# Attention scores cut into key chunks of 1024, 1024 and 256 in place of three of 768

## Chip, cores, metric

The kernel runs on one core of one Trainium2 chip, as one launch. The metric is device time in microseconds (us), the median of repeated runs. All matrix products here are done on operands split in two (a high part rounded to fp32r, and the rest), so that fp32 accuracy comes from two or three passes of fast matmuls.

## What is computed

One layer of a hybrid backbone for 128 prompt tokens and 2048 latent tokens, width 1024: RMS norm and modulation, one input projection, differential attention (8 heads) beside a bidirectional state-space scan (16 heads), one output projection, residual and final norm. The change is in the latent tokens' attention: 2048 queries against 2304 keys (2048 latent, 256 cached), per head two softmax maps of 64 dimensions each and values of 128.

```python
def diff_attention(q, k, v, lam):              # 8 heads, c = 2 maps of 64 dims
    ...
        s = jnp.einsum('bqhcd,bkhcd->bchqk', qi, k).astype(F32) * scale
        p = jax.nn.softmax(s, axis=-1)
        a = p[:, 0] - lam * p[:, 1]
        return jnp.einsum('bhqk,bkhd->bqhd', a.astype(v.dtype), v)
...
def layer(...):
    ...
    att = diff_attention(q, k_all, v_all, lam)
    ...
    out = jnp.concatenate([att, ssd_y], axis=-1) @ w_out
    return x + gate * out, ...
```

## The kernel before

The program goes through projections (TensorE tile ps_p), the scan (ps_y, ps_cb), the latent attention, and the output projection (ps_f). The body does not issue instructions: it records them, and a planner puts them in order. `Plan.simulate` (L388) walks the recorded instructions with an assumed cost for each (`Plan.price`, L305) and, engine by engine, takes of those that are ready the one that is due first. The result is one fixed order for each engine, which the chip follows: an engine whose next instruction has to wait does nothing else. Every recorded instruction carries the line L233, so the tiles' names tell them apart.

The latent attention has 128 units: 8 heads by 16 query tiles of 128 rows; two consecutive units make a pair that shares its queries (256) and its values' output. `frame(i)` (L1617) records unit i's scores beside the later steps of earlier units:

- `s_chunk` (L1509): scores of one map (m = 0, 1) against one key chunk (j = 0, 1, 2). TensorE writes them into tile ps_s, from the pool psS (L1473), which has two buffers of two PSUM banks; queries' high part and rest are two passes over the same keys (high parts in partitions 0 to 63, rests in 64 to 127 of the key tile K). VectorE evicts the chunk with one instruction (TENSOR_SCALAR, in the profile TENSOR_SCALAR_CACHE_REDUCE) into the SBUF tile S of that map and takes the chunk's row maximum on the way. Six chunks make a unit: three of map 0, three of map 1. Since the pool has two buffers, the matmuls of each chunk wait for the eviction of the chunk before the last.
- `s_max`, `s_exp`: the maximum over the chunks (VectorE), the exponential with its sum (ScalarE).
- `combine` (L1534): VectorE makes one factor (tile sm) from the sums, GpSimd forms map 0 minus lambda times map 1, in three pieces of 768 columns.
- `t_high`, `t_low` (L1545): TensorE transposes the result, three blocks of 128 at a time, into ps_t (three buffers, shared with ps_q); ScalarE takes the high part (aH), VectorE the rest (aL).
- `av_kt` (L1567): per block of 128 keys three value matmuls of 256 columns into ps_o, for both units of the pair at once.

`load_k` (L1373) loads one key chunk as one tile K by two DMAs on SP's queue, high parts and rests; nine tiles of 768 keys hold one and a half heads. The planner's cost of a score matmul is columns / 2.4 + 3 ns.

Of the kernel before, what the change touches and what calls it, by code (L numbers as in the profile page):

```python
# [9 lines left out]
F32 = mybir.dt.float32  # L10
F32R = mybir.dt.float32r
# [7 lines left out]
P = 128  # L19
D = 1024  # L20
KT = D // P
SEQ = 128
# [445 lines left out]
def body(tc, I, O):  # L468
    pl = Plan(tc)
    nc = pl  # L470
    es = ExitStack()
    mm = nc.tensor.matmul
# [76 lines left out]
    def bank(tag):  # L549
        return psB.tile([P, 512], F32, tag=tag, name=f"ps_{tag}", bufs=(1 if tag == "cb" else 2))  # L550
# [163 lines left out]
    for m0 in range(0, 2 * D, 384):  # L714
        n = min(384, 2 * D - m0)
# [13 lines left out]
    for g, wm in enumerate(wms):  # L729
# [3 lines left out]
        n = min(384, 2 * D - g * 384)  # L733
        if g in (2, 5):
            for j in range(2):
# [7 lines left out]
                for f in range(n // P):  # L743
                    o = 2 * (g * 3 + f) + j
                    mm(pm[:, o:o + 1], lhsT=acc[:, f * P:(f + 1) * P], rhs=ones[:, 0:1], start=True, stop=True)
            continue
        ps = bank("y")
# [4 lines left out]
        for f in range(n // P):  # L752
            o = 2 * (g * 3 + f)
# [614 lines left out]
    kpool_cm = pl.tile_pool(name="kpool", bufs=1, side="right", reuse_waits="tile")  # L1368
    kpool = kpool_cm.__enter__()
    NG = NKEY // 768  # L1370
    Kt, Vt = {}, {}

    def load_k(h, m, j):  # L1373
        t = kpool.tile([P, 768], F32R, tag="K", name="K", bufs=9)
        for r, src in enumerate((kH_d, kL_d)):
            load(out=t[r * 64:r * 64 + 64].bitcast(F32),
                 in_=src[h, m * 64:m * 64 + 64, SEQ + j * 768:SEQ + (j + 1) * 768])
        Kt[h, m, j] = t

    def load_q(h, t):  # L1380
# [8 lines left out]
    for m in range(2):  # L1389
        for j in range(NG):  # L1390
            load_k(0, m, j)
# [82 lines left out]
    psS = psS_cm.__enter__()  # L1474
# [24 lines left out]
    def get_unit(i):  # L1499
        if i not in U:  # L1500
            u = U[i] = Obj()
            u.pr = get_pair(i // 2)
            u.h, u.c, u.qo = i // 16, 1 + i % 16, (i % 2) * P
            u.pool = spS if i % 4 < 2 else spT
            u.S, u.mx = {}, u.pool.tile([P, 2, 4], F32, tag="mx", name="mx", bufs=2)
            u.sm = u.pool.tile([P, 4], F32, tag="sm", name="sm", bufs=2)
        return U[i]

    def s_chunk(i, k):  # L1509
        u = get_unit(i)  # L1510
        m, j = k // NG, k % NG
        if j == 0:
            u.S[m] = u.pool.tile([P, NKEY], F32, tag=f"S{m}", name=f"S{m}", bufs=2)
        ps = psS.tile([P, 2, 512], F32, tag="S", name="ps_s")
        kt = Kt[u.h, m, j]
        for l in range(2):
            for a in range(2):
                mm(ps[:, a, :384], lhsT=u.pr.q[:, l, m, u.qo:u.qo + P], rhs=kt[:, a * 384:(a + 1) * 384],
                   start=l == 0, stop=l == 1)
        src, dst = ps[:, :, :384], u.S[m][:, j * 768:(j + 1) * 768]  # L1520
        nc.vector.tensor_scalar(out=dst.rearrange("p (a b) -> p a b", a=2), in0=src, scalar1=1.0, scalar2=None,
                                op0=ALU.mult, op1=ALU.max, accum_out=u.mx[:, m, j:j + 1])

    def s_max(i):
        u = U[i]
        for m in range(2):
            nc.vector.tensor_reduce(out=u.mx[:, m, 3:4], in_=u.mx[:, m, 0:NG], axis=AX.X, op=ALU.max, negate=True)

# [5 lines left out]
    def combine(i):  # L1534
# [3 lines left out]
                                op0=ALU.mult, op1=ALU.mult)  # L1538
        for j in range(NG):
            sl = slice(j * 768, (j + 1) * 768)  # L1540
# [76 lines left out]
    def frame(i):  # L1617
# [12 lines left out]
        for k in range(6):  # L1630
            if live:
                s_chunk(i, k)
                h, r = i // 16, i % 16
                if r == 15 and h + 1 < NH and k >= 3:
                    load_k(h + 1, 1, k - 3)
                if r == 5 and h + 1 < NH and k < 3:
                    load_k(h + 1, 0, k)
                if r == 6 and h + 1 < NH and k < 2:
                    load_v(h + 1, k, 0)
            if tl:  # L1640
                t_high(ti, k)
                t_low(ti, k)
            if k % 2 == 0:
                av((i - 3) * 3 + k // 2 - 1)
# [27 lines left out]
    spT = spT_cm.__enter__()  # L1672
    for g in range(NG):
        for l in range(2):
# [202 lines left out]
```

## Time and profile before

| | |
|---|---|
| median of 3 runs | 3106.76 us (3104.68, 3106.76, 3111.84) |
| the profiled execution | 3110.01 us |
| its span, first to last instruction | 3108.1 us |
| mean granted TensorE clock, share of full speed | 0.994 |
| TensorE busy | 3054.7 us, 98% |
| VectorE, ScalarE, GpSimd busy | 2305.7, 1836.8, 1327.8 us |
| score matmuls, first and last start | 1480.1 and 2687.4 us |

The busy time of matmuls counts overlapping ones once; a row with "xN" merges N instructions, and its mean (ns of one) includes the part in which the next matmul already runs. How far apart matmuls follow each other is read from the chain or from a count over a stretch. PEld is the loading of a matmul's stationary operand.

### The profile page before, as it was taken

What the parts mean: (1) busy time and instruction counts of PE and PEld (TensorE: products, weight loads), DVE (VectorE), ACT (ScalarE), POOL (GpSimd) and SP (SyncE); (2) the same over time, 40 slices, a digit from 0 to 9 for tenths busy, and PEclk for the clock granted to TensorE, in tenths of its full rate; (3) what the DMA queues carried; (4) which work ended last, traced back from release to release, by engine and by line L of the source; (5) the groups of instructions that cost most, each with busy time, mean ns of one, the idle gap of its engine ahead of it and who ended that gap; (6) DMA issues with size and microseconds to landing.
All of it is one profiled execution on the core that took longest, in us unless ns stands there. A gap on an engine that the chain in (4) does not pass through costs nothing.

```text
span 3108.1 us, 55843 instructions
## 1 busy us (share of the span) xinstructions
PE 3054.7 (98%) x20539; PEld 2899.4 (93%) x20539; DVE 2305.7 (74%) x4638; ACT 1836.8 (59%) x3258; POOL 1327.8 (43%) x1171
## 2 busy tenths in 40 slices
PE   8999999999999999999999999999999999989999
PEld 5899999998999999998999999999999999868887
DVE  5544524767685777754799999999999999877775
ACT  3233313333475667744688888888888888754442
POOL 2010100000021222210699999999999999700000
PEclk9999999999999999999999999999999999999999
DMA  8632422677687777759222222222223121286663
GB/s 287 213 122 91 139 79 96 195 237 235 219 266 242 235 235 247 240 164 215 78 61 76 67 66 65 67 66 65 68 68 77 55 71 35 90 277 199 176 203 96
DMA packets 481474, 449.25 MB, mean 145 GB/s; under 512 B 34447, under 2 KB 437160, under 8 KB 481202
## 3 DMA queue, kind: packets, MB, share of 16 engines
q1 hardware_dynamic: 479282, 445.52, 47.2%
q8 instruction: 162, 2.65, 0.4%
q14 instruction: 110, 0.90, 0.1%
q10 hardware_dynamic: 1920, 0.17, 0.0%
HBM read 305.96 MB, written 139.62 MB: 143 GB/s over the span
## 4 chain that ended last, share of the span: by engine, by line
PE 87%; DMA 4%; DVE 4%; SPq 2%; issue 1%; ACT 1%; POOL 1%; DVEq 0%; POOLq 0%; ACTq 0%
PE ps_p L233 32%; PE ps_s L233 17%; PE ps_o L233 13%; PE ps_t L233 8%; PE ps_f L233 5%; PE ps_v L233 5%; PE ps_y L233 4%; DMA yL<-y_d 2%; SPq L233 2%; DVE yx L233 1%; PE ps_tr L233 1%; DVE o L233 1%; PE ps_cb L233 1%; DMA vH_d<-vH 1%; POOL st L233 0%
## 5 line engine op out<-in xcount | busy, mean ns | idle before, releaser
L233 DVE TENSOR_SCALAR_CACHE_REDUCE S<-ps_s 128x768 f32<-128x768 f32 x768 | 726.7, 953 | 64.3 <-PE ps_s L233 49.1
L233 POOL TENSOR_TENSOR S<-S,S 128x768 f32<-128x768 f32 x384 | 710.5, 1878 | 5.0
L233 PE MATMUL ps_s<-K,q 128*128 128x384 f32 x3072 | 707.7, 348 | 0.4 <-DVE S L233 0.2
L233 PE MATMUL ps_p<-hH,wH 128*128 128x384 f32 (+1 forms) x2112 | 697.9, 330 | 0.0
L233 PE MATMUL ps_p<-hH,wL 128*128 128x384 f32 (+1 forms) x2112 | 690.8, 327 | 0.0
L233 PE MATMUL ps_p<-hL,wH 128*128 128x384 f32 (+1 forms) x2112 | 689.7, 327 | 0.0
L233 ACT ACTIVATE S<-S,mx 128x2304 f32<-128x2304 f32 x256 | 571.0, 2230 | 11.8 <-DVE mx L233 11.8
L233 PEld LDWEIGHTS ps_s<-K,q 128*128 128x128 f32 x3072 | 505.7, 189 | 2.6 <-DVE S L233 2.0
L233 PE MATMUL ps_o<-aH,V 128*128 128x256 f32 x2304 | 490.9, 286 | 0.0
L233 ACT CAST aH<-ps_t 128x384 fp32r<-128x384 f32 x768 | 348.1, 482 | 135.1 <-PE ps_t L233 131.8
L233 DVE TENSOR_TENSOR aL<-ps_t,aH 128x384 fp32r<-128x384 f32 x768 | 406.4, 550 | 25.7 <-ACT aH L233 21.6
L233 POOL TENSOR_SCALAR_AFFINE_SELECT ar<-ar 128x512 f32<-128x512 f32 x136 | 111.2, 825 | 704.8 <-ACT ea L233 663.8
L233 PEld LDWEIGHTS ps_p<-hH,wH 128*128 128x128 f32 x2112 | 398.6, 189 | 2.0 <-issue 1.2
L233 PEld LDWEIGHTS ps_p<-hL,wH 128*128 128x128 f32 x2112 | 398.7, 189 | 1.0 <-issue 0.8
L233 PEld LDWEIGHTS ps_p<-hH,wL 128*128 128x128 f32 x2112 | 398.4, 189 | 0.7 <-DVE wL L233 0.3
L233 POOL TENSOR_SCALAR S<-S,sm 128x768 f32<-128x768 f32 x384 | 347.2, 922 | 86.9 <-DVE sm L233 77.4
L233 PEld LDWEIGHTS ps_o<-aH,V 128*128 128x128 f32 x2304 | 381.1, 189 | 0.2
L233 PE MATMUL ps_t<-cst,S 128*128 128x128 f32 x2304 | 355.6, 272 | 1.7 <-DVE aL L233 1.3
L233 PE MATMUL ps_o<-aL,V 128*128 128x256 f32 x1152 | 330.1, 287 | 0.0
L233 PEld LDWEIGHTS ps_t<-cst,S 128*128 128x128 f32 x2304 | 284.4, 140 | 17.1 <-DVE aL L233 1.7
L233 DVE TENSOR_TENSOR wL<-wr,wH 128x1024 fp32r<-128x1024 f32 x88 | 109.1, 1240 | 209.9 <-ACT wH L233 206.5
L233 PEld LDWEIGHTS ps_o<-aL,V 128*128 128x128 f32 x1152 | 218.2, 189 | 0.4 <-DVE aL L233 0.3
(246 smaller groups left out, 4724.5 us busy)
## 6 DMA issues: line engine op xcount, KB each, us to landing
wr<-in_w_in SPq DMA_DIRECT2D x88, 512.0 KB
ar<-row_d SPq DMA_DIRECT2D x68, 512.0 KB
q<-qH_d SPq DMA_DIRECT2D x128, 128.0 KB
q<-qL_d SPq DMA_DIRECT2D x128, 128.0 KB
xb<-xbc_d SPq DMA_DIRECT2D x17, 640.0 KB
K<-kH_d SPq DMA_DIRECT2D x48, 192.0 KB
K<-kL_d SPq DMA_DIRECT2D x48, 192.0 KB
V<-vH_d SPq DMA_DIRECT2D x24, 384.0 KB
```

Source lines behind the costliest of these rows:

```text
L233: getattr(e, name)(*[rl(v) for v in args], **{k: rl(v) for k, v in kw.items()})
```

## The change

Key chunks are 1024, 1024 and 256 wide; a key tile has the chunk's width (six tiles of 1024 and three of 256 take the room of nine of 768); score matmuls have 512 columns, and 256 in the last chunk. The eviction is one instruction per chunk as before, now over 1024 or 256 unbroken columns. The pool psS keeps its two buffers of two banks, and the small chunk takes a whole one. GpSimd's pieces of 768, the transposes and the value matmuls are as before.

```diff
--- before.py
+++ after.py
@@ -1368,13 +1368,15 @@
     kpool_cm = pl.tile_pool(name="kpool", bufs=1, side="right", reuse_waits="tile")
     kpool = kpool_cm.__enter__()
     NG = NKEY // 768
+    KGRP = ((0, 1024), (1024, 1024), (2048, 256))
     Kt, Vt = {}, {}
 
     def load_k(h, m, j):
-        t = kpool.tile([P, 768], F32R, tag="K", name="K", bufs=9)
+        o, n = KGRP[j]
+        t = kpool.tile([P, n], F32R, tag=f"K{n}", name=f"K{n}", bufs=6 if n > 256 else 3)
         for r, src in enumerate((kH_d, kL_d)):
             load(out=t[r * 64:r * 64 + 64].bitcast(F32),
-                 in_=src[h, m * 64:m * 64 + 64, SEQ + j * 768:SEQ + (j + 1) * 768])
+                 in_=src[h, m * 64:m * 64 + 64, SEQ + o:SEQ + o + n])
         Kt[h, m, j] = t
 
     def load_q(h, t):
@@ -1511,14 +1513,14 @@
         m, j = k // NG, k % NG
         if j == 0:
             u.S[m] = u.pool.tile([P, NKEY], F32, tag=f"S{m}", name=f"S{m}", bufs=2)
-        ps = psS.tile([P, 2, 512], F32, tag="S", name="ps_s")
+        ps = psS.tile([P, 1024], F32, tag="S", name="ps_s")
         kt = Kt[u.h, m, j]
+        o, n = KGRP[j]
         for l in range(2):
-            for a in range(2):
-                mm(ps[:, a, :384], lhsT=u.pr.q[:, l, m, u.qo:u.qo + P], rhs=kt[:, a * 384:(a + 1) * 384],
-                   start=l == 0, stop=l == 1)
-        src, dst = ps[:, :, :384], u.S[m][:, j * 768:(j + 1) * 768]
-        nc.vector.tensor_scalar(out=dst.rearrange("p (a b) -> p a b", a=2), in0=src, scalar1=1.0, scalar2=None,
+            for a in range(0, n, 512):
+                e = min(a + 512, n)
+                mm(ps[:, a:e], lhsT=u.pr.q[:, l, m, u.qo:u.qo + P], rhs=kt[:, a:e], start=l == 0, stop=l == 1)
+        nc.vector.tensor_scalar(out=u.S[m][:, o:o + n], in0=ps[:, :n], scalar1=1.0, scalar2=None,
                                 op0=ALU.mult, op1=ALU.max, accum_out=u.mx[:, m, j:j + 1])
 
     def s_max(i):
```

What the planner makes of it is shown at one place, where a unit goes from map 0 to map 1. TensorE before, in the middle of the attention (S_24436 is the unit two earlier, whose result is transposed in threes; the ps_s rows are, in turn, the second chunk of map 0, its third, and the first of map 1):

```order
L233 MATMUL ps_s<-K,q 128x384 x4
L233 MATMUL ps_t<-cst,S_24436 128x128 x3
L233 MATMUL ps_s<-K,q 128x384 x4
L233 MATMUL ps_o<-aH,V 128x256
L233 MATMUL ps_o<-aL,V 128x256
L233 MATMUL ps_o<-aH,V 128x256 x2
L233 MATMUL ps_o<-aL,V 128x256
L233 MATMUL ps_o<-aH,V 128x256 x2
L233 MATMUL ps_o<-aL,V 128x256
L233 MATMUL ps_o<-aH,V 128x256
L233 MATMUL ps_s<-K,q 128x384
```

The third chunk (x4) and nine value matmuls stand between the second chunk's end and the next chunk that takes its buffer. TensorE with the change, at a unit that comes once in six units (K_21925 is the second 1024 chunk of map 0, K_21973 its 256 chunk, K_23909 the first of map 1, which takes K_21925's buffer):

```order
L233 MATMUL ps_s<-K_21909,q 128x512 x2
L233 MATMUL ps_o<-aL,V 128x256
L233 MATMUL ps_o<-aH,V 128x256
L233 MATMUL ps_t<-cst,S_24440 128x128 x3
L233 MATMUL ps_s<-K_21925,q 128x512 x4
L233 MATMUL ps_t<-cst,S_24440 128x128 x3
L233 MATMUL ps_s<-K_21973,q 128x256 x2
L233 MATMUL ps_s<-K_23909,q 128x512 x3
L233 MATMUL ps_t<-cst,S_24440 128x128 x3
L233 MATMUL ps_o<-aH,V 128x256
```

Two matmuls of 256 columns and three transposes stand between; the value matmuls now follow behind three matmuls of the next chunk. In the units between, at this place, the cover is longer: the value matmuls stand ahead of the next chunk.

VectorE before, at such a place (S_24707 is map 0 of a unit, S_24778 its map 1; 128x768 are evictions, aL the subtractions of the transposes' rests):

```order
L233 TENSOR_SCALAR S_24707,mx<-ps_s 128x768
L233 TENSOR_TENSOR aL<-ps_t,aH 128x3x128 x2
L233 TENSOR_REDUCE mx<-mx 128x1
L233 TENSOR_SCALAR S_24707,mx<-ps_s 128x768 x2
L233 TENSOR_TENSOR aL<-ps_t,aH 128x3x128
L233 TENSOR_REDUCE mx<-mx 128x1
L233 TENSOR_SCALAR S_24778,mx<-ps_s 128x768
```

VectorE with the change, at the place shown for TensorE (S_24701 is map 0, its two 1024 chunks and its 256 chunk, S_24766 map 1):

```order
L233 TENSOR_REDUCE mx<-mx 128x1
L233 TENSOR_SCALAR S_24701,mx<-ps_s 128x1024
L233 TENSOR_TENSOR aL<-ps_t,aH 128x3x128
L233 TENSOR_SCALAR S_24701,mx<-ps_s 128x1024
L233 TENSOR_SCALAR S_24701,mx<-ps_s 128x256
L233 TENSOR_TENSOR aL<-ps_t,aH 128x3x128
L233 RECIPROCAL sm<-sm 128x1
L233 TENSOR_REDUCE mx<-mx 128x1
L233 TENSOR_SCALAR sm<-l1c,nlam,sm 128x1
L233 TENSOR_TENSOR aL<-ps_t,aH 128x3x128
L233 TENSOR_SCALAR S_24766,mx<-ps_s 128x1024 x2
```

One subtraction stands between the two 1024 evictions of map 0, none between the second and the small one.

## Rows read from the trace of the kernel before

**Rows 1.** The page's head and its part 1: busy time of each engine, its share of the span, instructions.
```profile
span 3108.1 us, 55843 instructions
...
PE 3054.7 (98%) x20539; PEld 2899.4 (93%) x20539; DVE 2305.7 (74%) x4638; ACT 1836.8 (59%) x3258; POOL 1327.8 (43%) x1171
```

**Rows 2.** Busy time of all engines (with their instruction counts) in the stretch 1600 to 2600 us, then the granted clock, the DMA engines' mean busy share and GB/s.
```profile
1600.00:2600.00 1000.00, 1000.00 (x7378) 987.75 (x7377) 933.58 (x2336) 822.88 (x1329) 942.22 (x744) 1.00 0.25 67
```

**Rows 3.** The waits of the stretch 1600 to 2600 us, all of them: who waited for whom, us in total, times, the longest.
```profile
ACT aH L233 <- PE ps_t L233: 104.1, 106, 1.2
ACT qr L233 <- PE ps_q L233: 69.4, 53, 1.4
POOL S L233 <- DVE sm L233: 48.0, 52, 1.0
DVE S L233 <- PE ps_s L233: 31.8, 53, 0.6
DVE aL L233 <- ACT aH L233: 17.6, 52, 0.5
POOL S L233 <- DVE aL L233: 1.2, 1, 1.2
PEld ps_q L233 <- POOL sqs L233: 0.2, 1, 0.2
DVE S L233 <- issue: 0.2, 1, 0.2
```

**Rows 4.** The stretch 1600 to 2600 us once more: the chain of work by tile, then the windows view of the score tile (ps_s), the value tile (ps_o) and the transposes' tile (ps_t), whose first count is that of matmuls.
```profile
by line: PE ps_s L233 44.5%; PE ps_o L233 34.0%; PE ps_t L233 20.8%; PE ps_q L233 0.7%
...
1600.00:2600.00 1000.00, 587.55 (x2548) 419.07 (x2549) 607.73 (x1274) 1.00 0.25 67
...
1600.00:2600.00 1000.00, 430.26 (x2869) 387.33 (x2867) 54.54 (x159) 1.00 0.25 67
...
1600.00:2600.00 1000.00, 294.24 (x1908) 235.62 (x1908) 337.30 (x638) 289.58 (x638) 1.00 0.25 67
```

**Rows 5.** Pieces of the chain in the output projection (start, us, what): matmuls of 512 columns of the same operand type, in batches of 96.
```profile
2802.24 21.87 PE ps_f L233 x96
...
2824.32 21.87 PE ps_f L233 x96
...
2846.41 21.87 PE ps_f L233 x96
```

**Rows 6.** VectorE's timeline around 2010 us (start, us, what), where it works without a break, and two of its groups over the whole span (busy, mean ns of one, idle before).
```profile
2009.58 0.56 DVE L233 TENSOR_TENSOR aL<-ps_t,aH 128x384 fp32r<-128x384 f32 x1 [0.34 <-ACT aH L233]
2010.05 0.95 DVE L233 TENSOR_SCALAR_CACHE_REDUCE S<-ps_s 128x768 f32<-128x768 f32 x1
2010.92 0.08 DVE L233 DVE_READ_ACCUMULATOR S<-ps_s 128x1 f32 x1
2010.92 0.95 DVE L233 TENSOR_SCALAR_CACHE_REDUCE S<-ps_s 128x768 f32<-128x768 f32 x1
...
L233 DVE TENSOR_SCALAR_CACHE_REDUCE S<-ps_s 128x768 f32<-128x768 f32 x768 | 726.7, 953 | 64.3 <-PE ps_s L233 49.1 <-issue 0.2
...
L233 DVE TENSOR_TENSOR aL<-ps_t,aH 128x384 fp32r<-128x384 f32 x768 | 406.4, 550 | 25.7 <-ACT aH L233 21.6
```

**Rows 7.** Timeline of the attention's ramp, where TensorE's weight load waits for an eviction, and VectorE for matmuls.
```profile
1481.20 0.96 DVE L233 TENSOR_SCALAR_CACHE_REDUCE S<-ps_s 128x768 f32<-128x768 f32 x1 [5.51 <-PE ps_s L233]
...
1482.22 0.65 PEld L233 LDWEIGHTS ps_s<-K,q 128*128 128x128 f32 x4 [0.16 <-DVE S L233]
1482.22 0.97 PE L233 MATMUL ps_s<-K,q 128*128 128x384 f32 x4
...
1483.19 0.87 PE L233 MATMUL ps_s<-K,q 128*128 128x384 f32 x4
1483.22 0.96 DVE L233 TENSOR_SCALAR_CACHE_REDUCE S<-ps_s 128x768 f32<-128x768 f32 x1 [0.18 <-PE ps_s L233]
```

**Rows 8.** Waits of the ramp, 1470 to 1560 us.
```profile
DVE S L233 <- PE ps_s L233: 12.9, 9, 5.5
...
PEld ps_s L233 <- DVE S L233: 1.8, 6, 0.5
```

**Rows 9.** SP's timeline as the next head's key tiles are issued, one piece of the chain at 2890 us, and the sizes of both kinds of transfer (count, KB each).
```profile
1621.62 0.47 SPq L233 DMA_DIRECT2D K<-kH_d  x1
1622.14 0.59 SPq L233 DMA_DIRECT2D K<-kL_d  x1
...
1634.17 0.49 SPq L233 DMA_DIRECT2D K<-kL_d  x1
...
2890.39 6.40 DMA yL<-y_d
...
K<-kH_d SPq DMA_DIRECT2D x48, 192.0 KB
...
yL<-y_d SPq DMA_DIRECT2D x17, 512.0 KB
```

## The prediction

> **What bounds the kernel now.** I read the page's head first, then the busy time of each engine over 1000 us of the latent attention, then the waits there, and last the chain and the timeline. TensorE is busy for 98% of the span [rows 1]. In the stretch 1600 to 2600 us it is busy all the time at a clock share of 1.00, with VectorE at 934, GpSimd at 942 and ScalarE at 823 us of the 1000, and DMA at a quarter [rows 2]. The list of waits of that stretch has no line in which matmuls wait for an eviction; what waits are VectorE, ScalarE and GpSimd, and their lines are short [rows 3]. So here TensorE sets the pace, and a time it does not work is lost. It does 2548 score matmuls in these 1000 us [rows 4], 24 to a unit (one query tile of 128 for one head), so a unit takes 1000 x 24 / 2548 = 9.42 us; there are 128 units.
>
> **TensorE's own work.** The columns stay: 24 x 384 = 16 x 512 + 4 x 256 = 9216 per unit. What falls is the number of matmuls, 24 to 20, so a cost per instruction counts. The chain gives 44.5% of the 1000 us to score matmuls: 445 / 2548 = 174.6 ns for 384 columns; and 34.0% to the value matmuls, 340 us for 2869: 118.5 ns for 256 columns [rows 4]. For 512 columns the nearest row is the output projection with the same operand type: 96 matmuls in 21.87 us, 227.8 ns [rows 5]. Before: 24 x 174.6 = 4190 ns per unit. After: 16 x 227.8 + 4 x 118.5 = 4119 ns. That is 71 ns less, over 128 units **9.2 us** less; the rounding of the shares is worth 0.6 us. The Trainium skill ("TensorE: Matmul & The Clock Gate", section "Wait — 56ns, not 53.3ns?") puts the fixed cost of a matmul at about 2.5 ns beside its columns, by which 512 matmuls fewer would give only 1.3 us. The rows disagree: from 384 to 512 columns is 53.2 ns, 0.416 ns a column, which leaves 14.9 ns per matmul, so I stay with 9.2.
>
> **VectorE's work.** A chunk stays one eviction, six to a unit. Back to back, a 384-wide subtraction holds the engine 0.47 us and a 768-wide eviction 0.87 us (starts at 2009.58, 2010.05, 2010.92) [rows 6]: 1.04 ns an element. So 1024 holds it 1.13 us and 256 0.34 us, and 4 x 1.13 + 2 x 0.34 = 5.20 replaces 6 x 0.87 = 5.22 us: nothing. What changes is when a buffer comes free: 768 takes 0.95 us from start to end, so 1024 takes 0.95 + 0.27 = 1.22 us and 256 some 0.42.
>
> **The new wait.** The score pool has two buffers of two banks, whatever the chunk's size, so chunk k+2 cannot start until chunk k is evicted. What covers that eviction is chunk k+1 and whatever else stands between in TensorE's order. With equal chunks, chunk k+1 is always four matmuls, 0.70 us. With the new cut the chunk behind the second 1024 is two matmuls of 256 columns, 0.24 us. By the order, most units have 1.6 us or more of work between a unit's second 1024 chunk of the first map and the first of the second map (typically 1.96 us), but in a steady rhythm every sixth unit has just three transposes and the small chunk there, since the nine value matmuls that stood at this place now come behind three of the next chunk's matmuls. There are 21 such units (20 in the rhythm, and one, with 0.68 us, in the ramp). Their cover: transposes take 20.8% of the 1000 us, 208 us for 1908, so 109 ns each [rows 4]; 3 x 109 + 2 x 118.5 = 0.56 us.
>
> What is to be covered: VectorE starts 0.03 us after the last matmul of a chunk (1482.22 + 0.97 to 1483.22); after an eviction's end (1481.20 + 0.96) the waiting weight load starts 0.06 us later, and the four matmuls behind it take 0.97 in place of 0.87 us [rows 7]. So 0.03 + 1.22 + 0.06 + 0.10 = 1.41 us, and 1.41 - 0.56 = 0.85 us is missing. VectorE may also come late: it has the eviction before (1.13) and a subtraction (0.47) to issue first, 0.03 + 1.60 = 1.63 us after the earlier chunk's end, while TensorE ends the next one 2 x 118.5 + 327 + 4 x 227.8 = 1.48 us after it; so it starts 1.63 - 1.51 = 0.12 us late. I take 0.95 us a place, between a lower end of 1.22 + 0.03 - 0.56 = 0.69 (no restart cost, VectorE punctual) and an upper end of 0.97 + 0.47 = 1.4 (one more subtraction late). 21 x 0.95 = **20.0 us** more (14 to 29). The Trainium skill ("Perfetto Trace Analysis", section "Optimizing Scalar/DVE Operations") says that where a vector engine that is not saturated causes bubbles on another, breaking its instructions up may help; this change does the opposite at four of six evictions.
>
> **The rest.** In the ramp the order has one more short place, 0.89 us of cover in the third unit: 0.5 us. Before, the ramp had 1.8 us of such waits already [rows 8]. Key tiles: as many DMAs and as many bytes, 256 and 64 KB each in place of 192. They are issued once the last unit of a head frees their buffer (from 1621.62 us on), and the earliest reuse is one and a half units later, 14 us; a transfer of 512 KB in a much busier stage kept the chain 6.40 us [rows 9]. Hidden: nothing, and if that cover were gone, seven head changes at a few us each. SP issues the same number, GpSimd and ScalarE have the same instructions, so their totals stay, but with GpSimd at 94% [rows 2] new waits of transposes for it, or for the transposes' three buffers while VectorE is in a long eviction, are possible. From below zero (all is absorbed, as before), from above 0.4 us per six units, 8 us. I take zero, as the waits of before show no line of transposes behind GpSimd.
>
> **Sum.** -9.2 + 20.0 + 0.5 = +11.3 us. Against the profiled execution, 3110.01 us with a span of 3108.1, that gives 3121.3. That execution lies 3.25 us above the median 3106.76 of the three runs (3104.68 to 3111.84), so against the median **3118 us**. A measurement can tell about 0.2%, 6.2 us, from no change.
>
> **Rivals.**
> - *Not slower: the wait is short.* If the unbroken 1024 run loses the fixed part of an eviction (0.95 - 0.80 = 0.15) and the restart costs nothing, a place costs 1.07 + 0.03 - 0.56 = 0.54 us, 11 us in all, +2: 3109. It breaks even at 9.2 / 21 = 0.44 us a place and shows as slower above 0.73. For it: one row only shows the restart. Against it: 0.95 us is what every one of 768 evictions takes [rows 6].
> - *Faster: TensorE does not meet the wait.* Then only the 9.2 us are left: 3097.6. For it: TensorE waited for nothing in 1000 us although VectorE was 93% busy. Against it: two buffers are a hard limit, and 0.56 us cannot hold an eviction of 1.22.
> - *GpSimd or the transposes' buffers join in.* VectorE's long evictions delay the scalar (sm) for which GpSimd already waits 48 us in 52 waits of the stretch [rows 3]; some 0.4 to 1 us more per six units, 20 times: +8 to +20, so 3126 to 3138.
> - *No cost per matmul.* If columns alone set the pace, fewer matmuls give nothing, and the waits are left: +20.5, 3127. Against it stand the 53 ns from 384 to 512 columns [rows 4, 5]. The skill's figure of 2.5 ns above goes this way.
> - *The change does not do what it says* has little room: the order shows 2048 matmuls of 512 and 512 of 256 columns.
>
> **How the numbers follow.** Forecast 0.58: 0.69 to 1.4 us a place, so +6 to +21, 3112 to 3128; with the runs' own spread of 7 us a fifth of this would read as no change. Short wait 0.13: no change. No wait met 0.13: faster. GpSimd 0.12 and no cost per matmul 0.04: slower. So faster 0.13, same 0.25 (0.13 and 0.12 from the forecast), slower 0.62. The range leaves out most of the faster case and the far end of the GpSimd case: 3099 to 3132; the forecast's own is 3112 to 3128.
>
> **What would show it.** In the changed profile: score matmuls at 227 to 228 ns for 512 columns; evictions of 1.22 and 0.42 us; a line of weight loads or score matmuls waiting for S on VectorE, some 20 times, 0.7 to 1 us each, once in six units (57 us), at the second map's first chunk; a unit of 9.35 us where there is none. It is wrong if that line is missing, if the waits are of transposes, if the waits come more often than each sixth unit, or if the time falls by some 9 us.

## The result, and the profile after

The changed kernel takes **3151.85 us** (median of 4 runs, 3149.83 to 3153.3) against 3106.75 us for the kernel before, run beside it: ratio 1.0141, 95% interval 1.0129 to 1.0153. That is 45 us slower. The prediction said slower, but 3118 us with a range to 3132. One execution each of kernels 1 and 14 below, and one of the kernel before beside kernels 1 to 4, ran at a lower granted clock; the ratios leave it out, the medians do not.

The page's head and part 1 of the changed kernel, then its busy times in 1600 to 2600 us (PE, PEld, DVE, ACT, POOL, clock, DMA share, GB/s):

```profile
span 3149.3 us, 55019 instructions
...
PE 3074.4 (98%) x20027; PEld 2800.0 (89%) x20027; DVE 2307.9 (73%) x4638; ACT 1836.7 (58%) x3258; POOL 1331.5 (42%) x1171
...
1600.00:2600.00 1000.00, 981.72 (x6699) 872.33 (x6699) 901.79 (x2251) 792.23 (x1280) 905.97 (x717) 1.00 0.24 65
```

The 512 matmuls are gone (20539 to 20027), the totals of VectorE, ScalarE and GpSimd are as before [rows 1], and in the stretch where TensorE was busy for all of 1000.00 us [rows 2] it now idles 18. That is less than the loss in this stretch, because a row's busy time reaches on into the work behind it: of the waits found below only the long ones leave a gap in it. The clock share is 1.00 in both. TensorE's waits of that stretch for scores' and transposes' buffers (total, times, longest), and VectorE's two evictions (busy, mean ns, idle before):

```profile
PEld ps_s L233 <- DVE S L233: 28.9, 51, 1.2
...
PE ps_s L233 <- DVE S L233: 16.3, 17, 1.0
...
PEld ps_t L233 <- issue: 8.0, 34, 0.2
...
L233 DVE TENSOR_SCALAR_CACHE_REDUCE S<-ps_s 128x1024 f32<-128x1024 f32 x410 | 498.2, 1221 | 67.9 <-PE ps_s L233 64.2 <-issue 0.4 <-PE ps_o L233 0.3
...
L233 DVE TENSOR_SCALAR_CACHE_REDUCE S<-ps_s 128x256 f32<-128x256 f32 x205 | 85.6, 417 | 0.0
```

The list of before had no line of TensorE waiting for S [rows 3]; now score weight loads wait 51 times in 1000 us, and transposes 34 times. 17 of the 51 are long ones (the 17 of the second row, in which TensorE itself stands still) and 34 short ones. The chain shows the rhythm (start, us, what):

```profile
1627.74 1.23 DVE S L233 x2
1629.45 1.15 DVE S L233 x2
...
1686.47 1.23 DVE S L233 x2
```

Once in 58.73 us, which is six units, the chain leaves TensorE and runs through two evictions on VectorE, with a subtraction of 0.47 us between them. Six units took 6 x 9.42 = 56.5 us before [rows 4]; 2.2 us more, 21 times, are 46 us, the loss. Where these 2.2 us are lost is seen in two timelines. **The long wait**, TensorE and VectorE at 2039 to 2042 us:

```profile
2038.92 1.18 PE L233 MATMUL ps_s<-K,q 128*128 128x512 f32 x4
2039.94 0.49 PE L233 MATMUL ps_t<-cst,S 128*128 128x128 f32 x3
2040.18 0.48 PE L233 MATMUL ps_s<-K,q 128*128 128x256 f32 x2
2041.63 0.97 PE L233 MATMUL ps_s<-K,q 128*128 128x512 f32 x3 [0.96 <-DVE S L233]
...
2041.63 0.53 PEld L233 LDWEIGHTS ps_s<-K,q 128*128 128x128 f32 x3 [1.17 <-DVE S L233]
...
2038.73 1.22 DVE L233 TENSOR_SCALAR_CACHE_REDUCE S<-ps_s 128x1024 f32<-128x1024 f32 x1 [0.16 <-PE ps_s L233]
...
2039.88 0.55 DVE L233 TENSOR_TENSOR aL<-ps_t,aH 128x384 fp32r<-128x384 f32 x1
2040.35 1.22 DVE L233 TENSOR_SCALAR_CACHE_REDUCE S<-ps_s 128x1024 f32<-128x1024 f32 x1
```

The second 1024 chunk of the first map ends at 2038.92 + 1.18 = 2040.10. VectorE, in order behind the eviction before and a subtraction, starts its eviction 0.25 us later and ends at 2041.57; 0.06 us later the weight load of the next map's first chunk starts. The three matmuls that then stand in one row take 0.97 us, of which 3 x 0.232 is their pace. 0.27 us is beyond it: 0.10 is the restart (the second matmul starts 0.337 us behind the first, by the trace's single starts), and 0.17 is the overhang of a last matmul's end over its pace. The chunk before the wait has it too: it ends at 2040.10, the transposes behind it start at 2039.94. So 0.25 + 1.22 + 0.06 + 0.27 - 0.57 of cover (three transposes, two matmuls of 256 columns) = **1.23 us** lost, at the predicted place.

**The two short waits**, 2003 to 2007 us:

```profile
2003.28 1.09 PE L233 MATMUL ps_s<-K,q 128*128 128x512 f32 x4
2004.21 0.49 PE L233 MATMUL ps_t<-cst,S 128*128 128x128 f32 x3
2004.45 1.18 PE L233 MATMUL ps_s<-K,q 128*128 128x512 f32 x4
2005.46 0.28 PE L233 MATMUL ps_o<-aH,V 128*128 128x256 f32 x1
2005.69 0.50 PE L233 MATMUL ps_s<-K,q 128*128 128x256 f32 x2
2006.25 0.52 PE L233 MATMUL ps_t<-cst,S 128*128 128x128 f32 x3
...
2004.40 1.23 DVE L233 TENSOR_SCALAR_CACHE_REDUCE S<-ps_s 128x1024 f32<-128x1024 f32 x1 [0.39 <-PE ps_s L233]
...
2005.56 0.55 DVE L233 TENSOR_TENSOR aL<-ps_t,aH 128x384 fp32r<-128x384 f32 x1
...
2005.69 0.30 PEld L233 LDWEIGHTS ps_s<-K,q 128*128 128x128 f32 x2 [0.27 <-DVE S L233]
...
2006.22 0.31 PEld L233 LDWEIGHTS ps_t<-cst,S 128*128 128x128 f32 x3 [0.23 <-issue]
```

The small chunk of the second map needs the buffer of that map's first chunk; its cover is three transposes, four matmuls of 512 columns and one value matmul, 0.33 + 0.93 + 0.12 = 1.37 us, and the eviction ends at 2005.63: 0.22 us lost (from the value matmul's end at 2005.74 to 2006.19 are 0.45 us for two matmuls of 0.119). Right behind it, three transposes wait for their third buffer, which the subtraction at 2005.56, queued behind the same eviction, sets free at 2006.11: 2006.77 - 2006.19 - 0.33 = 0.25 us. Both happen twice in six units. 1.23 + 2 x 0.22 + 2 x 0.25 = 2.17 us in six units, 46 us over 21.

### The profile page after: what moved, and what is told of

Read it like the earlier page. It is cut to its first block, busy times and chain, and to the rows that moved or that the text cites. A ratio compares the mean times of both kernels' runs of the same rounds, so it can differ in the third digit from the quotient of the medians.

```text
span 3149.3 us, 55019 instructions
## 1 busy us (share of the span) xinstructions
PE 3074.4 (98%) x20027; PEld 2800.0 (89%) x20027; DVE 2307.9 (73%) x4638; ACT 1836.7 (58%) x3258; POOL 1331.5 (42%) x1171
## 4 chain that ended last, share of the span: by engine, by line
PE 91%; DMA 3%; DVE 3%; SPq 1%; ACT 1%; POOL 1%; issue 0%; DVEq 0%; POOLq 0%; ACTq 0%
PE ps_p L233 32%; PE ps_s L233 17%; PE ps_o L233 13%; PE ps_f L233 11%; PE ps_t L233 8%; PE ps_v L233 5%; PE ps_y L233 3%; DVE S L233 2%; PE ps_tr L233 1%; SPq L233 1%; PE ps_cb L233 1%; DMA vH_d<-vH 1%; DMA wraw<-in_w_out 1%; DMA wm<-in_w_mod 0%; DMA K<-kL_d 0%
## 5 line engine op out<-in xcount | busy, mean ns | idle before, releaser
L233 DVE TENSOR_SCALAR_CACHE_REDUCE S<-ps_s 128x1024 f32<-128x1024 f32 (+1 forms) x768 | 717.8, 953 | 92.3 <-PE ps_s L233 87.7
L233 PE MATMUL ps_s<-K,q 128*128 128x512 f32 (+1 forms) x2560 | 708.3, 386 | 20.6 <-DVE S L233 20.6
L233 PE MATMUL ps_o<-aH,V 128*128 128x256 f32 x2304 | 511.6, 291 | 1.0 <-ACT aH L233 1.0
L233 PEld LDWEIGHTS ps_s<-K,q 128*128 128x128 f32 x2560 | 423.6, 189 | 79.3 <-DVE S L233 36.7
L233 PE MATMUL ps_t<-cst,S 128*128 128x128 f32 x2304 | 371.6, 272 | 2.5 <-POOL S L233 0.2
```

What stands on the lines that cost most here:

```text
L233: getattr(e, name)(*[rl(v) for v in args], **{k: rl(v) for k, v in kw.items()})
```

## The experiments

Each was compared with the kernel before, run beside it on the same chip (its medians 3108.7 to 3112.2 us), so runs are compared with each other by their ratios. The theory: evictions of 1024 at two buffers make these waits. Rivals: the matmuls of 512 columns themselves, VectorE's busy time, the order alone.

**1. One bank for each matmul's columns, an eviction per 512.**
```
-psS bufs=2, ps = psS.tile([P, 1024])       one eviction [:n] per chunk
+psS bufs=4, ps = psS.tile([P, 512]) per a   one eviction [:e - a] per a, right behind its two matmuls
```


> Key tiles of 1024, 1024 and 256 and matmuls of 512 columns as in the change, but each 512 columns get a buffer of one bank (four buffers) and an eviction of their own, ten to a unit in place of six. Theory: the 45 us are TensorE waiting for evictions of 1.22 us from two buffers; with evictions of some 0.69 us and four buffers those waits go, and the time is within 3 us of the kernel before, 3104 to 3110 if a score matmul of 512 columns stays at 232 ns, about 3098 if it falls to 228. Rival, that the planner's new order costs the time whatever the buffers: 3130 or more. Rival, that VectorE is at its limit: ten evictions cost it 0.27 us a unit more, and the time goes to 3120 or above.

Measured: 3109.37 us, ratio 0.9991 (0.9981 to 1.0001). Its windows of all engines, and its chain by line with the count of score matmuls, 1600 to 2600 us:

```profile
1600.00:2600.00 1000.00, 1000.00 (x6952) 906.44 (x6951) 957.77 (x3185) 822.57 (x1329) 938.52 (x743) 1.00 0.25 67
...
by line: PE ps_s L233 44.5%; PE ps_o L233 34.0%; PE ps_t L233 20.9%; PE ps_q L233 0.6%
...
1600.00:2600.00 1000.00, 587.31 (x2126) 339.93 (x2125) 644.72 (x2124) 1.00 0.25 67
```

TensorE is busy all the time again, with the same key tiles and matmuls, although VectorE works more (958 against 902). So the waits, not the matmuls or VectorE's load, are the 45 us. This kernel changes the number of buffers, the evictions' length and the order together; it does not say which of them takes the waits away. And the gain of fewer matmuls isn't there: 445 us for 2126 matmuls, 20 to a unit, are 4.19 us a unit, as before (24 x 174.6 ns). With the 424 matmuls of 256 columns at 0.119 us, the 1702 others take 232 ns each.

**2. The two banks of a chunk one after the other.**
```
-        for l in range(2):
-            for a in range(0, n, 512):
+        for a in range(0, n, 512):
+            for l in range(2):
```

> The change, with the two passes (high part, rest) into one bank behind each other, then the next bank, in place of bank by bank in each pass. Theory of the bank: a score matmul of 512 columns takes 232 ns for its change of bank at each matmul; it falls to 228 ns and the time by some 8 us, to 3144. Rival, that the 4 ns come from something else: 232 ns and 3152 as for the change.

Measured: 3152.27 us, 1.0131 (1.0115 to 1.0147). The order of the banks within a chunk plays no part.

**3 and 4. The small chunk in a buffer of its own, which takes a bank from the transposes; and, as a control, the kernel before with two transposes' buffers.**
```
3  +ps of a chunk of 256: psS.tile([P, 512], tag="S3", bufs=1)
3, 4  -psT bufs=3
3, 4  +psT bufs=2
```

> The change, with the 256 chunk in a buffer of its own (one bank), so that the next 1024 chunk no longer waits for the last one's eviction; the transposes have two buffers in place of three to make room. Theory: no wait of some 1.2 us behind the small chunk, score matmuls wait for VectorE less than 5 us in all; transposes' waits for their two buffers come instead, as in the kernel before with two. Time of the change less 26 to 35 us if those are small: 3117 to 3126. Rival, that the small chunk's place is not the cause: 3150 or more.

> The kernel before with two buffers for transposes in place of three: what the room for the small chunk's buffer costs by itself. If the third buffer is hardly used, 3107 to 3112; if transposes then wait for VectorE, 3130 or more, and the run beside it is to be read against this one.

Measured: 3184.11 us, 1.0235 (1.0219 to 1.0251), and 3175.71 us, 1.0208 (1.0192 to 1.0224). The transposes' third buffer is worth 65 us by itself. Kernel 3 missed its forecast: score loads should hardly have waited, and in 1600 to 2600 us they wait 121 times, in the changed kernel 51:

```profile
PEld ps_s L233 <- DVE S L233: 46.6, 121, 0.7
```

Against its control the cut costs 8 us in place of 45, but both kernels are full of other waits, so the pair does not test the small chunk's place.

**5. Chunks of 768 in matmuls of 512 and 256 columns** (from the kernel before).
```
-ps = psS.tile([P, 2, 512])     for a in range(2): mm(ps[:, a, :384], ...)
+ps = psS.tile([P, 1024])       for a, e in ((0, 512), (512, 768)): mm(ps[:, a:e], ...)
```

> The kernel before with its chunks of 768 keys, each now in matmuls of 512 and 256 columns in place of two of 384; buffers, evictions and key tiles as before. Theory (places and evictions of 1024 make the loss; a score matmul of 512 columns costs about 232 ns here): no waits for evictions, and 12 x (232 + 119) = 4212 ns a unit against 24 x 174.6 = 4190, so +2.8 us, about 3110 us. If a 512-column score matmul costs the 227.8 ns of the output projection: 12 x (227.8 + 118.5) = 4156, -4.4 us, about 3102 to 3104. Rival (matmuls of 512 columns themselves, or their two banks written unequally, bring the waits): near the changed kernel, 3150.

Measured: 3113.71 us, 1.0005 (0.9996 to 1.0014), TensorE busy 1000.00 of 1000 us. Its chain by line and its count of score matmuls:

```profile
by line: PE ps_s L233 44.5%; PE ps_o L233 34.0%; PE ps_t L233 20.8%; PE ps_q L233 0.6%
...
1600.00:2600.00 1000.00, 557.23 (x2540) 387.59 (x2538) 606.05 (x1271) 1.00 0.24 67
```

24 matmuls to a unit take 445 / 2540 x 24 = 4.20 us: 512 and 256 columns cost what two of 384 cost, and the 512 alone 350 - 119 = 231 ns. Matmuls of 512 columns bring no waits, and in equal chunks there are none.

**6. GpSimd nearly idle** (kernel 1, in `combine`), to see whether its traffic stretches the 512-column matmuls.
```
-            sl = slice(j * 768, (j + 1) * 768)
+            sl = slice(j * 768, j * 768 + 64)
```

> The kernel with one bank for each score matmul of 512 columns and an eviction each (four buffers), in which GpSimd combines only the first 64 of each 768 probabilities of a unit; the rest is left out, so GpSimd is almost idle in the attention. It is run for the pace of a 512-column score matmul alone: 231 to 232 ns in that kernel with GpSimd 94% busy, 227.8 in the output projection. If GpSimd's traffic in on-chip memory slows TensorE's reads: 228 ns or so. If not: 231 to 232 again, and the time stays within 0.3%, as TensorE sets the pace.

Measured: 3108.33 us in one run. By line and the busy time of all engines:

```profile
by line: PE ps_s L233 44.4%; PE ps_o L233 34.0%; PE ps_t L233 20.9%; PE ps_q L233 0.6%
...
1600.00:2600.00 1000.00, 1000.00 (x6955) 907.36 (x6954) 951.17 (x3186) 820.17 (x1326) 266.86 (x742) 1.00 0.25 67
```

GpSimd works 267 us in place of 939, and the scores keep their share. What holds the 512-column score matmul at 232 ns, when the output projection does the same shape in 227.8 [rows 5], stays open.

**7 to 11. Other orders.** In five runs the changed kernel got another order of its instructions, by other prices in the planner or, in the second, by an eviction that is two instructions (both behind the chunk's four matmuls).

```
7  matmul in the attention:  max(m/2.4, 107) + 3   ->  max(m/2.4 + 14.5, 109)
8  eviction of 1024:         one tensor_scalar      ->  two of 512, in a row
9, 10  eviction of scores:   + 500 ns; + 200 ns
11 every ScalarE operation in the attention: + 250 ns
```

> The changed kernel with one other price in the planner: a matmul costs its columns / 2.4 + 14.5 ns, at least 109, as measured, in place of the greater of columns / 2.4 and 107, plus 3. It moves the order only: what stands between the second 1024 chunk of the first map and the first of the second map is 1.01 us of TensorE's work in every second unit (63 places) and nowhere less, in place of 0.56 us in every sixth; the two places of 1.37 us in six units are gone. Theory (places in the order times what their cover lacks): an eviction needs 0.03 + 1.22 + 0.06 + 0.27 = 1.58 us, with up to 0.25 more where VectorE is late, so 0.57 to 0.82 us are missing at each place, 36 to 52 us, about 3142 to 3160 us, with waits of that length every second unit. Rival (the loss is a rhythm of the engines that the order does not decide, VectorE's long evictions as such): the same three kinds of waits and 3150 again, with waits of 1.2 us. Rival (the waits come from the planner's wrong price): about 3107.

> The changed kernel with its two buffers of two banks and its four matmuls a chunk, but each 1024 chunk is evicted by two instructions of 512 columns, both behind the four matmuls. That makes the eviction longer, 0.68 + 0.68 = 1.37 us for 1.22, and the planner, which prices it, writes another order: the second 1024 chunk of the first map has now at least 1.96 us of TensorE's work behind it in the steady rhythm, and the least cover of a 1024 chunk there is 1.64 to 1.70 us, two or three times in six units. Theory (places times what their cover lacks): a need of 0.03 + 1.37 + 0.06 + 0.27 = 1.73 us, so waits of at most 0.1 us, some 0.3 in six units, 6 us in all: 3107 to 3120 us, although every eviction is longer. Rival (the length of the evictions, or VectorE's busy time, as such sets the loss): 0.15 us more on each of the waits that the changed kernel has, 100 in all, so 3160 to 3170 us.

> The changed kernel; the planner's price of an eviction of scores is raised by 500 ns, so it writes another order and nothing else differs. Counted along TensorE's order with the paces measured in the changed kernel (232, 119, 109 ns a matmul, evictions of 1.22 and 0.42 us in turn, 0.33 us from an eviction's end to the pipeline's pace): the cover of a second 1024 chunk of the first map never falls below 1.6 us in the steady rhythm, but in 62 places it is 1.6 to 1.9 us with VectorE a little late, 0.15 us a place, 10.7 us in all; no short place for the value matmuls' buffer. Theory (the order's covers set the loss, eviction by eviction): 3115 to 3128 us. Rival (VectorE's long evictions cost TensorE their time whatever the order): 3150. Rival (the planner, with a worse price, only moves the wait to the value matmuls or transposes, as in the two kernels with other orders): 3130 to 3160.

> As the one with 500 ns, with 200 ns. Counted along its order: no place of the steady rhythm lacks cover (1.5 us of waits in all, in the ramp), and the value matmuls' one buffer has at least 2 us everywhere; the transposes' buffers have 1.96 us at 63 places, the shortest of all these orders. Theory: 3107 to 3117 us, so two buffers and evictions of 1024 cost next to nothing where the order covers them. Rival (long evictions as such): 3150. Rival (the wait moves to the transposes, 0.2 to 0.4 us at 63 places): 3120 to 3135.

> The changed kernel; the planner's price of every ScalarE operation in the attention is raised by 250 ns, so it writes another order and nothing else differs. Counted along its order: 185 places where a 1024 chunk's cover is below 1.6 us, with 0.2, 0.5 and 0.7 us missing in each period of two units, 84 us of waits in all. Theory (the order's covers set the loss): 3180 to 3200 us. Rival (long evictions as such, whatever the order): 3150. Rival (other waits, not the scores', set the loss; here the value matmuls' buffer has 3 us everywhere): about 3107 to 3120.

Measured: 3155.03 us (1.0142, 1.0128 to 1.0155), 3137.41 (1.0084, 1.0071 to 1.0098), 3279.75 (1.0542, 1.0527 to 1.0558), 3194.26 (1.0264, 1.0248 to 1.0279) and 3219.78 (1.0342, 1.0324 to 1.0359). Kernel 7 fell within its forecast, for another reason than the one given; the other four missed theirs. Waits of TensorE in 1600 to 2600 us, first of kernel 7:

```profile
PEld ps_o L233 <- ACT sq L233: 26.0, 51, 0.5
```

There the value matmuls wait for ScalarE to empty their one buffer, and the scores' eviction ends meanwhile (at 2003.12 us a value matmul starts after such a wait, the eviction ends at 2003.19, the score matmul starts at 2003.34). Of kernel 8 (two evictions):

```profile
PEld ps_o L233 <- DVE aL L233: 10.2, 16, 0.6
```

Its waits have no line of score loads or score matmuls behind an eviction: with the same two buffers, evictions that are longer (by 0.07 us, see kernel 14) and another order, that wait is gone, as forecast, and by the ratios the kernel is 18 us faster than the changed one. What is left are mainly value matmuls that wait for VectorE and ScalarE, which the forecast did not have. Of kernel 9 (+500 ns):

```profile
DVE sm L233 <- ACT S L233: 93.8, 186, 1.1
...
PEld ps_t L233 <- POOL S L233: 76.2, 139, 0.7
...
PEld ps_s L233 <- DVE S L233: 57.8, 93, 0.7
```

Of kernel 10 (+200 ns):

```profile
PEld ps_t L233 <- POOL S L233: 48.8, 98, 0.5
...
PEld ps_s L233 <- DVE S L233: 10.4, 50, 0.2
```

And of kernel 11 (ScalarE + 250 ns):

```profile
PEld ps_s L233 <- DVE S L233: 47.7, 97, 0.7
...
PEld ps_t L233 <- POOL S L233: 17.7, 48, 0.4
```

The covers counted along TensorE's order alone don't predict the time: in the last three orders transposes wait for GpSimd, and in kernel 9 VectorE, which waits in its queue for a sum of ScalarE (the first row of kernel 9), comes to its evictions later than the count assumes. The rival of waits that move elsewhere holds in kind, and in kernels 9 and 10 is far larger than its forecast. These runs compare orders, and say nothing on the length of an eviction. They do say that the size of the loss belongs to the order too: against the kernel before the five lose 43, 25, 168, 83 and 108 us.

**12 to 15. The order kept, the eviction changed.** In these four the planner was given the old price, so every engine keeps the changed kernel's order; only VectorE's eviction of 1024 columns differs.
```
12, 13  tensor_scalar(out=S[:, o:o + w], in0=ps[:, :w]); memset(S[:, o + w:o + n])      w = 768; 512
14      tensor_scalar of [0:512], then of [512:1024], both behind the four matmuls
15      as 14, the matmuls of the first bank ahead of those of the second
```

> The changed kernel with every engine's order exactly as it is there (the planner is given the old price), but an eviction of 1024 columns carries only the first 768; the other 256 columns of the scores' tile are set to zero by a memset right behind it, so the buffer comes free 0.27 us earlier. A quarter of the scores of these chunks is left out. Theory (at a given order the waits are what the eviction lacks in cover): the first kind of wait falls from 1.23 to 0.7 to 0.96 us at 22 places, the second (0.22 us at 40) and the third (0.25 us at 41) vanish, if the memset is short: 3107 + 17 to 23, so 3122 to 3132 us. Rival (at this order the waits do not depend on the eviction's length, as other engines are late): 3145 to 3152.

> As the one with 768, with 512: half the scores of these chunks is left out, and the buffer comes free 0.54 us earlier than in the changed kernel. Theory: a need of 0.03 + 0.68 + 0.06 + 0.27 = 1.04 us against 0.56 of cover, 0.48 us at 22 places and nothing else, 11 us: 3115 to 3122 us. Rival (independent of the eviction's length): 3145 to 3152.

> The changed kernel with every engine's order exactly as it is there; an eviction of 1024 columns is two instructions of 512 in a row, behind the chunk's four matmuls, 0.15 us longer together. Nothing is left out. Theory: 0.15 to 0.30 us more at each place of the three kinds, 1.38 to 1.53 us at 22, 0.37 to 0.52 at 40, 0.40 to 0.55 at 41: 64 to 77 us with the ramp, 3170 to 3187 us. Rival (independent of the eviction's length): 3152. Rival (two instructions free the first bank early): below 3145.

> As the one with two evictions in a row, but a chunk's matmuls finish one bank before they start the other, so the first eviction can start while TensorE is on the second bank; engines' orders otherwise as in the changed kernel, and nothing is left out. VectorE works as long as in that one. Theory: from a chunk's end to its buffer's release it is now 0.03 + 0.68 us where VectorE is free in time, so the first kind of wait is 0.03 + 0.68 + 0.33 - 0.56 = 0.48 us at 22 places, up to 0.9 where VectorE is late, and the others vanish: 11 to 20 us, 3118 to 3130 us. Rival (VectorE's busy time as such): at or above the kernel with two evictions in a row, 3152 to 3187.

Measured: 3141.85 us (1.0105, 1.0090 to 1.0120), 3139.28 (1.0099, 1.0084 to 1.0114), 3158.24 (1.0156, 1.0139 to 1.0173) and 3157.9 (1.0155, 1.0138 to 1.0172). None is where the theory had it (the last lies where its rival had it), and the waits say why. Of the kernel with 768: its waits, then VectorE at the place of the short waits:

```profile
PEld ps_s L233 <- DVE S L233: 14.4, 17, 0.8
PEld ps_t L233 <- issue: 13.6, 34, 0.4
PE ps_s L233 <- DVE S L233: 10.9, 17, 0.6
...
PE ps_t L233 <- DVE aL L233: 7.7, 34, 0.2
...
1998.41 0.96 DVE L233 TENSOR_SCALAR_CACHE_REDUCE S<-ps_s 128x768 f32<-128x768 f32 x1 [0.40 <-PE ps_s L233]
...
1999.38 0.27 DVE L233 MEMSET S<- 128x256 f32 x1
1999.57 0.49 DVE L233 TENSOR_TENSOR aL<-ps_t,aH 128x384 fp32r<-128x384 f32 x1
```

Score loads and score matmuls in the waits of the kernel with 512:

```profile
PEld ps_s L233 <- DVE S L233: 9.9, 17, 0.6
PE ps_s L233 <- DVE S L233: 6.4, 17, 0.4
```

And of the one with two evictions in a row, with VectorE at one such pair:

```profile
PE ps_s L233 <- DVE S L233: 19.0, 17, 1.1
...
2037.91 0.68 DVE L233 TENSOR_SCALAR_CACHE_REDUCE S<-ps_s 128x512 f32<-128x512 f32 x1
...
2038.52 0.68 DVE L233 TENSOR_SCALAR_CACHE_REDUCE S<-ps_s 128x512 f32<-128x512 f32 x1
```

*The long wait follows the eviction.* TensorE's idle time at the 17 places is 0.38, 0.64, 0.96 and 1.12 us for evictions of 0.69, 0.96, 1.22 and twice 0.68 us. From 1.22 to 0.96 it falls by 0.32, from there to 0.69 by 0.26: about one for one. Two in a row end 1.29 us after the first began, 0.07 more than one of 1024, where the forecast had 0.15; the wait grows by 0.16, about twice 0.07, and two such evictions stand in VectorE's queue there. In time this shows hardly: the ratios 1.0156 and 1.0141 have overlapping intervals.

*The first short wait follows it too:* it is gone in the kernels with 768 and 512, where score loads wait 17 times, and 51 times in the changed kernel.

*The second doesn't, since the edit left it.* The subtraction starts 1999.57 - 1998.41 = 1.16 us after the eviction did, exactly as in the changed kernel (2004.40 to 2005.56): the memset fills the time that the eviction gave up. The transposes wait till almost the same moment, now 0.4 us as nothing holds TensorE before them; the last row of waits names the subtraction. That is what the forecasts from 3122 and 3115 us missed; the first had said "if the memset is short". With it the two times come out: 22 long waits of 0.64 + 0.27 and 41 of 0.4 are 36 us (33 measured), 22 of 0.38 + 0.27 and 41 of 0.4 are 31 (31 measured).

*The last run tells nothing of its own:* its edit does not do what it was meant to. Chunk and eviction there, TensorE and VectorE:

```profile
2033.63 1.32 PE L233 MATMUL ps_s<-K,q 128*128 128x512 f32 x6
...
2034.76 0.69 DVE L233 TENSOR_SCALAR_CACHE_REDUCE S<-ps_s 128x512 f32<-128x512 f32 x1 [0.59 <-PE ps_s L233]
```

Six matmuls stand in the row (four of 512, two of 256); the first bank is complete some 0.17 + 2 x 0.232 us after 2033.63, at 2034.26, but VectorE, idle, starts when all four of 512 are through. It waited for the whole buffer, and the kernel's waits are those of the kernel with two in a row.

## Why the prediction was wrong

- **What bounds the kernel, and the direction: right.** TensorE sets the pace, and a wait that it meets is lost.
- **The place: right.** 17 long waits in 1000 us, once in six units, between the small chunk of the first map and the first chunk of the second; evictions of 1.22 and 0.42 us, as worked out.
- **The gain of 9.2 us: failed.** It priced the 512-column score matmul by the output projection's 227.8 ns. In the attention it takes 231 to 232 (kernels 1 and 5), so 16 x 232 + 4 x 119 = 4188 ns a unit against 4190: nothing. 4 ns in 228 were nearly the whole term, and a row from another stage doesn't have them. Its own rows of the attention pointed this way: from 256 to 384 columns they have 56.1 ns [rows 4], which carried on to 512 gives 230.7 ns and a gain of 3 us. So the rival *no cost per matmul* came true in its effect: 20 matmuls take as long as 24. From 256 to 384 columns are 55.7 ns, from 384 to 512 57.4, 0.435 and 0.448 ns a column, where the forecast had 0.416 and put the rest on each matmul. By the Trainium skill ("TensorE: Matmul & The Clock Gate", section "Wait — 56ns, not 53.3ns?"), with 2.5 ns per matmul, the gain would have been an estimated 1.3 us. The measured gain, 0.3 us where the shares' rounding is worth 0.6, cannot tell that from nothing. A single matmul's time disagrees with it: 232 ns are 18.7 more than 512 columns at 2.4 GHz.
- **0.95 us a place: mis-sized; it is 1.23.** Of the missing 0.28 us, 0.17 is the overhang. The forecast compared two rows of four matmuls, 0.97 and 0.87 us [rows 7], and took 0.10, which is the restart and was right. But it counted the need from the end of the chunk's last matmul and the cover by paces from where the next work starts, and the end lies 0.17 us later. Both rows held it: 0.87 - 4 x 0.175 = 0.17. Most of the rest is VectorE: it starts 0.25 us after the chunk's end where 0.03 + 0.12 was reckoned with, and 0.95 was taken where the terms add up to 0.97. 21 places and a shorter one in the ramp are 26 us, for 20.5.
- **Two kinds of wait were missed, 19 us** (40 places of 0.22 and 41 of 0.25, by the counts in the forecast of kernel 12). The second map's small chunk is not in the prediction, which counts covers at one place of a unit only: with its need of 1.41 us the cover of 1.37 would have lacked 0.04 us, with the overhang 0.21, and 0.22 were measured. The transposes' buffers were named with a bound of 8 us and taken at zero, because the list of before had no line of them. Their subtraction stands behind the same evictions. This half of the rival *GpSimd or the transposes' buffers* came true, without GpSimd.
- **The sum.** 11.3 + 9.2 + 6 + 19 = 45.5, against 45 measured.
- The Trainium skill ("Perfetto Trace Analysis", section "Optimization Strategy") reads a gap that repeats on the engine that should be saturated as a possible lack of PSUM for the next tile, by buffer count or tile size. The runs agree: the gap comes each 58.7 us, and four buffers of one bank remove it (3109). Its other advice, to break up instructions of an engine that causes bubbles (section "Optimizing Scalar/DVE Operations"), brought the time back only together with smaller buffers (kernel 1): two evictions from one two-bank buffer gave 3158 us in the changed kernel's order and 3137 in the order that the planner wrote for them.

## What to carry to other kernels

With two buffers, equal chunks are what gives each eviction a cover of its own size; a small chunk between large ones takes that cover away wherever the order puts nothing else there, so cut the buffer with the tile, or keep chunks equal. Size a wait by all that stands ahead of the release in the releasing engine's queue, plus the last matmul's overhang and the restart, and look for every buffer that the same engine sets free behind it. A gain of 2% on one instruction must be priced from that instruction in its own stage.

## What was not expected of the hardware

A 512-column matmul of this operand type takes 227.8 ns in the output projection and 232 in the attention, with GpSimd busy or nearly idle; the cause is open. The long wait cost TensorE 0.33 us that are neither cover nor VectorE's: 0.06 from the eviction's end to the weight load, 0.10 at the first matmul behind the wait, and 0.17 by which a matmul's end lies behind its pace. A memset of 256 columns on VectorE took 0.27 us from start to end and 0.19 to the next instruction's start; the eviction had taken 0.27 us for them.
